# Router logits with the weights stationary in four column groups of TensorE, summed by a second product

## The chip, the cores and the metric

The kernel runs on one core of one Trainium2 chip. The metric is the device time of one execution in microseconds (us), taken as the median of several runs. Before the change it is 1420.48 us (three runs, 1419.78 to 1422.85).

## What is computed

One decoder layer on 256 tokens of width 1024, in float32: three parallel causal mixers (gated DeltaNet, a gated linear recurrence, sliding-window attention), merged and projected; a layer norm; a mixture of 32 experts of which every token uses four; a layer norm; a per-layer embedding; a layer norm. The change lies between the first layer norm and the experts, in the router:

```
x = layer_norm(DEEPNORM_ALPHA * x + y, ln1_g, ln1_b)          # y: the mixers' output, times w_out
logits = (xt @ router_w + router_b).astype(jnp.float32)       # (256, 1024) @ (1024, 32)
top_vals, top_idx = lax.top_k(logits, TOP_K)
gates = jax.nn.softmax(top_vals, axis=-1)
```

Every chosen pair of token and expert gets a seat in that expert's buffer, and the expert's two matrices are applied to the buffer.

## The kernel before

The program has two halves. The **mixer** half runs as a list of "units": each is a batch of matrix products (lines L396 and L406, each float32 operand split into a high and a low part, three products) into a PSUM tile `pjt`, and then a generator that evacuates the result. Beside the units run "strands", generators that are advanced once per unit (`steps` in `run`, L465 to L482). A `yield` in a generator therefore puts what follows it one unit later in the program, and when the units have run out the strands go round in turn until all are finished. The order of the instructions on each engine is fixed when the program is built; an engine executes its own queue strictly in that order.

The last nine units multiply the merged mixer output by `w_out`. The tokens come as two halves of 128 (t = 0, 1), the 1024 output columns as two halves of 512 (c = 0, 1). When one pair (t, c) is complete, `evac` in `out_unit` (L1196 to L1217) adds the residual (L1202, tile `y`), takes its statistics (L1203) and spawns `logits(t, c)` (L1219). That strand turns the 128 x 512 piece by four transposes (L1223), copies it from PSUM to the tile `xT` (L1224, printed under its buffer's name `MG`) on ScalarE, and multiplies it with the router's weights `rw`, whose rows were scaled by the norm's gain earlier (`router_weights`). Four products (L1228) per piece, each with 128 tokens of `xT` stationary and the 32 columns of `rw[:, k]` moving, accumulate the 128 x 32 logits of a half of the tokens in a PSUM bank `M["rps", t]`. The layer norm's mean and scale are put in afterwards, on the logits (L1259, L1260).

`router` (L1241) is one strand for both halves. On VectorE it takes for each t the logits (L1259, L1260), the four largest (L1262 to L1265, the choice goes into `tail`), and after an exponential on ScalarE (L1267) the softmax (L107 to L109). For t = 0 it then multiplies the choice with a triangular matrix (L1272) to count seats, and VectorE makes the seats (L118, L119) and the one-hot matrix `oh` (L113). `first_norm(t)` writes the normed tokens `xs` on ScalarE (L1238).

The **expert** half begins with `group(0)` (L1505): it gathers the seated tokens by products with the one-hot matrices (L1518; t = 0 first, then the seats of t = 1 by L123 to L126, L118, L119, L113, and then the gather with t = 1), scales them into `xe` (L1488), and then every expert does its first product (L1564), activation, second product (L1599) and the spread back (L1622). The weights, 12 MB for each expert, come through ten buffers of 2 MB, issued by SyncE (SP) in order. Two 512 KB transfers for the residual (`ob`, `bd`, L1527) are issued by ScalarE's queue.

Of the kernel before, what the change touches and what calls it, by code (L numbers as in the profile page):

```python
# [8 lines left out]
F32 = mybir.dt.float32  # L9
# [5 lines left out]
ALU = mybir.AluOpType  # L15
# [5 lines left out]
P = 128  # L21
KD = D // P
H = 8
NE = 32
# [39 lines left out]
def body(ctx, tc, nc, a, out, dbg=None):  # L64
    sync, act, dve, pool, pe = nc.sync, nc.scalar, nc.vector, nc.gpsimd, nc.tensor
    dbg = dbg or {}

    con = ctx.enter_context(tc.tile_pool(name="con", bufs=1))
    dram = ctx.enter_context(tc.tile_pool(name="dram", bufs=1, space=DRAM))
    pp = ctx.enter_context(tc.tile_pool(name="pp", bufs=1))  # L70
    cst = con.tile([P, 4 * P], F32, name="cst")
    ones = con.tile([P, P], F32, name="ones")

    con.tile([P, 96], F32, name="padc")
    xs = pp.tile([P, 2, D], F32, name="xs")
    rt = Routing(pp)
    pp.tile([P, 112], F32, name="padp")
    el = ctx.enter_context(tc.tile_pool(name="el", bufs=1))
    with ExitStack() as mx:
        mx.enter_context(tc.manual_schedule(engines=None))  # L80
        early = mixer(mx, tc, nc, a, xs, rt, dram, cst, ones, el)
    if dbg:
        for n, v in (("X1", xs), ("G", rt.G), ("POS", rt.pos)):
            pool.dma_start(dbg[n], v)
    moe(ctx, tc, nc, a, out, dbg, xs, rt, dram, cst, ones, el, early)
# [53 lines left out]
def mixer(mx, tc, nc, a, xs, rt, dram, cst, ones, el):  # L139
# [5 lines left out]
    sync, act, dve, pool, pe = nc.sync, nc.scalar, nc.vector, nc.gpsimd, nc.tensor  # L145
# [6 lines left out]
    m2 = mx.enter_context(tc.tile_pool(name="m2", bufs=2))  # L152
# [40 lines left out]
    rw = mpa.tile([P, KD, NE], F32, name="rw")  # L193
# [3 lines left out]
    mv = mpa.tile([P, 2, 4], F32, name="mv")  # L197
# [7 lines left out]
    def wait(*names):  # L205
        while not all(n in events for n in names):
            yield
# [16 lines left out]
    ident, stri, iota, cmask = (cst[:, i * P:(i + 1) * P] for i in range(4))  # L224
# [269 lines left out]
    M = {}  # L494
# [664 lines left out]
    lc_ = mpa.tile([P, 2, NE], F32, name="lc1")  # L1159

    def router_weights():
        yield from wait("late", "att3")
        col = lambda i: pr[:, 65 + 8 * i:73 + 8 * i].unsqueeze(2).to_broadcast([P, KD, NE])
        rb_ = m2.tile([P, T], F32, name="rwb", tag="sq").rearrange("p (k e) -> p k e", e=NE)
        sums_ = m2.tile([P, T], F32, name="rws", tag="sq").rearrange("p (n e) -> p n e", e=NE)
        dve.tensor_tensor(out=rb_, in0=rw, in1=col(1), op=ALU.mult)
        dve.tensor_reduce(out=sums_[:, 1], in_=rb_.rearrange("p k e -> p e k"), axis=AX.X, op=ALU.add)
        yield
        dve.tensor_tensor(out=rw, in0=rw, in1=col(0), op=ALU.mult)
        dve.tensor_reduce(out=sums_[:, 0], in_=rw.rearrange("p k e -> p e k"), axis=AX.X, op=ALU.add)  # L1170
        yield
        ps = yield from banks.take()
        pe.matmul(ps[:, 0:2 * NE], ones, sums_[:, 0:2].rearrange("p n e -> p (n e)"), start=True, stop=True)
        yield
        dve.tensor_scalar(lc_[:, 0], ps[:, 0:NE], -1.0, None, op0=ALU.mult)
        dve.tensor_add(lc_[:, 1], ps[:, NE:2 * NE], rb)
        banks.done(ps)
# [8 lines left out]
    def out_unit(work, done):  # L1186
# [10 lines left out]
        def evac(_):  # L1197
            for t, c in done:
                if t not in rows:
                    rows[t] = wp.tile([P, KD * P], F32, name="y", tag="w")  # L1200
                y = rows[t][:, halves[c]]
                dve.scalar_tensor_tensor(y, xs[:, t, halves[c]], 2.0 * ALPHA, out_ps[t, c], ALU.mult, ALU.add)  # L1202
                dve.bn_stats(lns[:, t, c], y)  # L1203
                if c == 0 and t == 0:
                    for i in range(2):
                        M["rps", i] = yield from banks.take()
                    M["wk"] = wp.tile([P, KD * P], F32, name="wk", tag="w")
                    pool.memset(M["wk"][:, 0:80], -3.0e38)
                spawn(logits(t, c))
                if c:  # L1210
                    dve.bn_aggr(mv[:, t, 0:2], lns[:, t])
                    dve.tensor_scalar(mv[:, t, 2:3], mv[:, t, 1:2], 4 * LN_EPS, None, op0=ALU.add)
                    pool.tensor_tensor(out=mv[:, t, 2:3], in0=mv[:, t, 2:3], in1=mhalf[:, 0:1], op=ALU.pow)
                    spawn(first_norm(t))
            yield
        return products, evac, ()

    def logits(t, c):

        xT = M["xT"]  # L1220
        b = yield from banks.take()
        for k in range(4):
            pe.transpose(b[:, k * P:(k + 1) * P], rows[t][:, (4 * c + k) * P:(4 * c + k + 1) * P], ident)  # L1223
        act.copy(xT[:, 4 * c:4 * c + 4, t * P:(t + 1) * P], b.rearrange("p (k t) -> p k t", k=4))  # L1224
        banks.done(b)
        yield
        for k in range(4 * c, 4 * c + 4):
            pe.matmul(M["rps", t][:, :NE], xT[:, k, t * P:(t + 1) * P], rw[:, k], start=k == 0, stop=k == KD - 1)  # L1228
        if c:
            events.add(f"r{t}")  # L1230

    def first_norm(t):
# [9 lines left out]
    def router():  # L1242

        yield from wait("r0", "n0")
        wk = M["wk"]
        n = [0]

        def take(c, rows=P):
            n[0] += c
            return wk[:rows, n[0] - c:n[0]]  # L1250
        two = lambda v: v.rearrange("p (t c) -> p t c", t=2)
        lg, mr40 = two(take(80)), two(take(80))
        ex, sel = (take(NE), rt.ex), (rt.sel0, rt.sel)
        m8, m4, sm = two(take(16)), two(take(16)), (take(2), rt.sm)
        pool.memset(m4, -3.0e38)
        for t in range(2):
            if t:
                yield from wait("r1", "n1")
            dve.scalar_tensor_tensor(lg[:, t, :NE], lc_[:, 0], mv[:, t, 0:1], M["rps", t][:, :NE], ALU.mult, ALU.add)  # L1259
            dve.scalar_tensor_tensor(lg[:, t, :NE], lg[:, t, :NE], mv[:, t, 2:3], lc_[:, 1], ALU.mult, ALU.add)  # L1260
            banks.done(M["rps", t])
            dve.max(m8[:, t], lg[:, t, :NE])  # L1262
            dve.tensor_copy(m4[:, t, 0:4], m8[:, t, 0:4])
            dve.match_replace(mr40[:, t], m4[:, t], lg[:, t], imm_value=-1.0e38)
            dve.tensor_tensor(out=sel[t], in0=mr40[:, t, :NE], in1=lg[:, t, :NE], op=ALU.not_equal)  # L1265
            dve.tensor_scalar(sm[t][:, 0:1], m8[:, t, 0:1], -1.0, None, op0=ALU.mult)
            act.activation(ex[t], lg[:, t, :NE], AF.Exp, bias=sm[t][:, 0:1])  # L1267
            if t == 0:
                rt.softmax(dve, 0, ex[0], sel[0], sm[0][:, 1:2])
                yield  # L1270
                ps2 = yield from banks.take()
                pe.matmul(ps2[:, :NE], stri, sel[0], start=True, stop=True)  # L1272
                yield
                rt.seat(dve, 0, ps2[:, :NE], sel[0])
                banks.done(ps2)
                rt.places(dve, iota, 0, 0)
# [87 lines left out]
    spawn(delta(1))  # L1364
    spawn(norm_rows())
    spawn(router_weights())
    spawn(router())
    spawn(prefetch())
    spawn(bias_parts())
# [521 lines left out]
```

## Time and profile before

| | us |
|---|---|
| median of three runs | 1420.48 |
| lowest and highest | 1419.78, 1422.85 |
| the profiled execution's own time | 1418.43 |
| its span, first to last instruction | 1416.70 |

The profile is of one execution. A row of the order of time gives a start, how long the row was busy, the engine, the line, the operation, what is written and read, the shape and how many instructions are merged into it; brackets at the end give the idle time before it and what ended it. PE is TensorE's products, PEld its loads of stationary operands, DVE VectorE, ACT ScalarE. A float32 product appears as two records, so the four products of a piece are a row of eight. The duration of a product's record holds its way through the array, so that rows overlap: the pace is read from one row's start to the next one's. The mixer half ends at about 443 us and the expert half fills the rest to about 1376 us.

### The profile page before, as it was taken

To read this page: it belongs to the slowest core of one execution; us is meant where nothing else is said; L and a number is where in the kernel's file an instruction comes from. 1 tells how busy PE (TensorE), PEld (TensorE's weight loads), DVE (VectorE), ACT (ScalarE), POOL (GpSimd) and SP (SyncE) were. 2 spreads that over 40 slices of the span, in tenths; PEclk is the share of its full clock that TensorE was granted. 3 is DMA by queue.
4 is the path that set the end of the run, shared out by engine and by line. 5 is a ranking of instruction groups with operands and counts; after the bars stand their busy time and mean duration, and the time that the engine had idled before them with its cause. 6 is when DMAs were issued, how large, how long until landed. Compare 5 with 4: busy or idle time off the path is not lost. (4 is left out here: it accounts for less than half of the span.)

```text
span 1416.7 us, 19387 instructions
## 1 busy us (share of the span) xinstructions
PE 1342.9 (95%) x7722; PEld 750.8 (53%) x7723; DVE 591.8 (42%) x1255; ACT 403.1 (28%) x811; POOL 250.0 (18%) x219
## 2 busy tenths in 40 slices
PE   8999989999999999999999999999999999999987
PEld 7989967888886333333333333334333333333326
DVE  6398884876564332223222222223222322222238
ACT  6767464644554111111111111111111111111121
POOL 6654774434561000000000000000000000000000
PEclk9999999999999999999999999999999999999988
DMA  8755455345887999999999999999999999999970
GB/s 263 216 139 137 132 183 170 111 139 181 308 302 281 414 429 431 429 429 428 428 431 429 430 428 427 431 430 429 427 430 430 430 429 427 430 429 430 429 295 30
DMA packets 122198, 481.69 MB, mean 340 GB/s; under 512 B 11403, under 2 KB 69404, under 8 KB 88696
## 3 DMA queue, kind: packets, MB, share of 16 engines
q1 hardware_dynamic: 120440, 477.16, 84.2%
q0 software_dynamic: 912, 1.87, 0.4%
q10 hardware_dynamic: 752, 1.38, 0.3%
q8 instruction: 62, 1.02, 0.3%
q14 instruction: 32, 0.26, 0.0%
HBM read 478.79 MB, written 3.42 MB: 340 GB/s over the span
## 5 line engine op out<-in xcount | busy, mean ns | idle before, releaser
L1564 PE MATMUL gu<-w,xe 128*64 128x512 f32 x1168 | 261.9, 599 | 0.0
L457 POOL TENSOR_TENSOR LO<-w,HI 128x384 fp32r<-128x384 f32 (+1 forms) x113 | 170.6, 1511 | 161.1 <-ACT HI L452 154.8
L1564 PE MATMUL gu<-F,xe 128*64 128x512 f32 x880 | 198.4, 596 | 0.1
L1564 PEld LDWEIGHTS gu<-w,xe 128*64 128x64 f32 x1168 | 82.9, 138 | 156.6 <-issue 153.2
L455 DVE TENSOR_TENSOR LO<-w,HI 128x640 fp32r<-128x640 f32 (+1 forms) x113 | 117.6, 1042 | 81.4 <-ACT HI L452 79.5
L1461 POOL DMA_DIRECT2D pt<-in_p_dram x1 | 0.8, 777 | 779.8 <-DVE lc L1586 779.8
L1627 DVE TENSOR_TENSOR Y<-Y,cb 128x512 f32<-128x512 f32 x128 | 82.1, 682 | 127.5 <-PE cb L1622 127.5
L452 ACT CAST HI<-w 128x1024 fp32r<-128x1024 f32 x113 | 118.0, 1045 | 59.1 <-PE pjt L406 35.1
L1599 PE MATMUL dn<-w,hT 128*64 128x512 f32 x560 | 132.2, 615 | 2.0 <-ACT hT L1592 2.0
L1582 DVE TENSOR_SCALAR gc<-gu 128x256 f32<-128x256 f32 x64 | 26.9, 421 | 249.3 <-PE gu L1564 249.3
L396 PE MATMUL pjt<-xh,HI 128*128 128x256 f32 x424 | 125.9, 297 | 0.0
L396 PE MATMUL pjt<-xh,LO 128*128 128x256 f32 x424 | 121.6, 287 | 1.3 <-DVE LO L455 1.3
L396 PE MATMUL pjt<-xl,HI 128*128 128x256 f32 x424 | 121.2, 286 | 0.0
L1564 PEld LDWEIGHTS gu<-F,xe 128*64 128x64 f32 x880 | 60.8, 137 | 112.8 <-issue 109.8
L1496 PE MATMUL gat<-oh,xs 128*128 128x128 f32 x480 | 72.3, 296 | 37.7 <-DVE oh L113 19.9
L1599 PE MATMUL dn<-F,hT 128*64 128x512 f32 x464 | 106.0, 599 | 0.0
L1583 ACT ACTIVATE sg<-gc 128x256 f32<-128x256 f32 x64 | 27.2, 425 | 274.6 <-DVE gc L1582 274.6
L1496 PEld LDWEIGHTS gat<-oh,xs 128*128 128x128 f32 x480 | 60.9, 199 | 55.4 <-issue 26.4
L396 PEld LDWEIGHTS pjt<-xh,HI 128*128 128x128 f32 x424 | 82.7, 195 | 1.8 <-issue 1.1
L396 PEld LDWEIGHTS pjt<-xh,LO 128*128 128x128 f32 x424 | 82.6, 195 | 2.0 <-DVE LO L455 1.9
L396 PEld LDWEIGHTS pjt<-xl,HI 128*128 128x128 f32 x424 | 82.7, 195 | 0.3
L1599 PEld LDWEIGHTS dn<-w,hT 128*64 128x64 f32 x560 | 38.2, 142 | 74.6 <-issue 63.5
(417 smaller groups left out, 1724.9 us busy)
## 6 DMA issues: line engine op xcount, KB each, us to landing
w<-in_w_gu_dram SPq DMA_DIRECT2D x73, 2048.0 KB, 26.9
F<-in_w_gu_dram SPq DMA_DIRECT2D x51, 2048.0 KB, 28.2
w<-in_w_down_dram SPq DMA_DIRECT2D x70, 1024.0 KB, 21.7
F<-in_w_down_dram SPq DMA_DIRECT2D x58, 1024.0 KB, 22.1
w<-in_w_in_dram SPq DMA_DIRECT2D x85, 512.0 KB, 3.8
F<-in_w_gu_dram SPq DMA_DIRECT2D x8, 1024.0 KB, 6.1
w<-in_w_o_lru_dram SPq DMA_DIRECT2D x8, 512.0 KB, 4.6
w<-in_w_o_swa_dram SPq DMA_DIRECT2D x8, 512.0 KB, 3.7
```

The lines of the kernel that those rows point to most:

```text
L396: pe.matmul(ps, hl[l][:, k * P:(k + 1) * P], b[r][:, k], start=k == 0 and n == 0, stop=k == KD - 1 and n == 2)
L452: act.copy(hi, s)
L455: dve.tensor_sub(lo[:, 0:n], s[:, 0:n], hi[:, 0:n].bitcast(F32))
L457: pool.tensor_tensor(out=lo[:, n:], in0=s[:, n:], in1=hi[:, n:].bitcast(F32), op=ALU.subtract)
L1461: pool.dma_start(pt, a["p"][0, 0].rearrange("(t p) c -> p t c", p=P))
L1496: pe.matmul(ps[:, kk], xs[:, t, k * P:(k + 1) * P], oh[:, t], start=t == 0, stop=t == 1)
L1564: pe.matmul(gu[64 * j:64 * j + 64, b], xe[:, k], w[:, j * D + b * 512:j * D + (b + 1) * 512], start=False, stop=k == KD - 1)
L1582: dve.tensor_scalar(gc[:, c], guv[:, c, 0], 7.0, None, op0=ALU.min)
L1583: act.activation(sg[:, c], gc[:, c], AF.Sigmoid, scale=1.702)
L1599: pe.matmul(dn[64 * jj:64 * jj + 64], hT[:, 2 * hf + kk, j * 64:j * 64 + 64], w[:, kk, jj * 512:(jj + 1) * 512], start=hf == j == kk == 0, ...
L1627: dve.tensor_add(y, y, pss[jj])
```

## The change

The products are turned round: `rw[:, k]` (128 x 32) is stationary and 128 tokens of `xT` move. The four products of a piece go to four groups of 32 columns of the array and so to four groups of 32 partitions of the bank, each holding a partial sum of the logits, transposed (32 experts x 128 tokens). When both pieces of a half are in, ScalarE copies the 128 x 128 partial sums to SBUF (tile `lgp`, L1239 of the changed kernel), and one product with that copy stationary and `sel4` moving (four 32 x 32 identities on top of each other) adds the four groups and turns the logits back to tokens x experts (L1242). `sel4` is built once, in the strand `router_weights`, by three additions on VectorE into a tile that was padding. For t = 0 the copy comes one unit later than the products and the sum one unit after the copy; for t = 1 there is no `yield` between them.

```diff
-    pp.tile([P, 112], F32, name="padp")
+    rt.odd = pp.tile([P, 112], F32, name="odd")
...
     def router_weights():
         yield from wait("late", "att3")
+        M["sel4"] = s4 = rt.odd[:, 16:48]
+        dve.tensor_add(s4, ident[:, 0:32], ident[:, 32:64])
+        dve.tensor_add(s4, s4, ident[:, 64:96])
+        dve.tensor_add(s4, s4, ident[:, 96:128])
...
         banks.done(b)
         yield
-        for k in range(4 * c, 4 * c + 4):
-            pe.matmul(M["rps", t][:, :NE], xT[:, k, t * P:(t + 1) * P], rw[:, k], start=k == 0, stop=k == KD - 1)
+
+        for k in range(4):
+            pe.matmul(M["rps", t][32 * k:32 * k + 32, 0:P], rw[:, 4 * c + k], xT[:, 4 * c + k, t * P:(t + 1) * P], start=c == 0, stop=c == 1)
         if c:
+
+            if t == 0:
+                yield
+            part = m2.tile([P, P], F32, name="lgp", tag="cv")
+            act.copy(part, M["rps", t][:, 0:P])
+            if t == 0:
+                yield
+            pe.matmul(M["rps", t][:, P:P + NE], part, M["sel4"], start=True, stop=True)
             events.add(f"r{t}")
...
-            dve.scalar_tensor_tensor(lg[:, t, :NE], lc_[:, 0], mv[:, t, 0:1], M["rps", t][:, :NE], ALU.mult, ALU.add)
+            dve.scalar_tensor_tensor(lg[:, t, :NE], lc_[:, 0], mv[:, t, 0:1], M["rps", t][:, P:P + NE], ALU.mult, ALU.add)
```

The change also moves work on three engines, because the strand `router` starts on an event that now comes two units later.

**VectorE, around the last piece (t = 1, c = 1).** L1202 and L1203 are that piece's residual and statistics, L1259 (changed kernel: L1272) the first step on the logits of t = 0, L109 the last of its softmax, L118 the first step of its seats. Before:

```order
L1259 SCALAR_TENSOR_TENSOR wk<-lc_150,mv,pg 128x32
L1260 SCALAR_TENSOR_TENSOR wk<-wk,mv,lc_150 128x32
...
L109 TENSOR_SCALAR GP<-wk 128x32
L1202 SCALAR_TENSOR_TENSOR y<-xs,pjt 128x512
L1203 BN_STATS lns<-y 128x6
L1211 BN_AGGR mv<-lns 128x2
L1212 TENSOR_SCALAR mv<-mv 128x1
L118 SCALAR_TENSOR_TENSOR GP<-pg,tail 128x32
```

Here the softmax of t = 0 is over before the last piece's residual begins. With the change:

```order
L1206 SCALAR_TENSOR_TENSOR y<-xs,pjt 128x512
L1207 BN_STATS lns<-y 128x6
L1215 BN_AGGR mv<-lns 128x2
L1216 TENSOR_SCALAR mv<-mv 128x1
L1272 SCALAR_TENSOR_TENSOR wk<-lc_150,mv,pg 128x32
L1273 SCALAR_TENSOR_TENSOR wk<-wk,mv,lc_150 128x32
...
L109 TENSOR_SCALAR GP<-wk 128x32
L1248 SCALAR_TENSOR_TENSOR mv<-mv 128x1
L118 SCALAR_TENSOR_TENSOR GP<-pg,tail 128x32
```

The chain of t = 0 stood ahead of the last piece's residual and now stands behind its statistics.

**ScalarE, at the same place.** L1224 (L1228) are the copies of turned pieces, L1267 (L1280) the exponentials, the first for t = 0 (`wk`), the second for t = 1 (`tail`). Before:

```order
L1224 COPY MG<-pg 128x4x128
L1267 ACTIVATE wk<-wk 128x32
L1224 COPY MG<-pg 128x4x128
L1238 ACTIVATE xs<-y,mv 128x512 x2
L1267 ACTIVATE tail<-wk,tail 128x32
```

The two middle rows are the exponential of t = 0 and, behind it, the last piece's copy. With the change:

```order
L1228 COPY MG<-pg 128x4x128
L1239 COPY lgp<-pg 128x128
L1280 ACTIVATE wk<-wk 128x32
L1228 COPY MG<-pg 128x4x128
L1239 COPY lgp<-pg 128x128
L1251 ACTIVATE xs<-y,mv 128x512 x2
L1280 ACTIVATE tail<-wk,tail 128x32
```

The order of the old instructions is the same, with two copies of partial sums put in; the exponential of t = 0 is still ahead of the last piece's copy.

**TensorE, from the last batch of products on.** L1272 (L1285) counts the seats of t = 0, L1518 (L1531) is the first gather. Before:

```order
L1272 MATMUL pg<-tail,cst 128x32
L1223 MATMUL pg<-cst,y 128x128 x4
L1548 LDWEIGHTS pick
...
L1548 MATMUL gu<-bias,pick 64x512
L1228 MATMUL pg<-rw,MG 128x32 x4
L1518 MATMUL gat<-oh_72,xs 128x128 x8
```

The count of the seats of t = 0 comes first, before the last piece is turned. With the change:

```order
L1242 MATMUL pg<-odd,lgp 128x32
L1227 MATMUL pg<-cst,y 128x128 x4
L1561 LDWEIGHTS pick
...
L1561 MATMUL gu<-bias,pick 64x512
L1285 MATMUL pg<-tail,cst 128x32
L1233 MATMUL pg<-MG,rw 32x128 x4
L1242 MATMUL pg<-odd,lgp 128x32
L1531 MATMUL gat<-oh_72,xs 128x128 x8
```

The sum for t = 0 stands where the count of its seats stood, and that count has moved behind the last piece's transposes and the expert half's first bias products.

## Rows read from the trace of the kernel before

**Rows 1.** Busy time by stretch: us, then PE PEld DVE ACT POOL (instructions), PEclk, DMA share, GB/s

```profile
445.00:450.00 5.00, 3.96 (x37) 3.43 (x33) 3.19 (x20) 3.37 (x5) 0.60 (x2) 1.00 0.98 419
600.00:700.00 100.00, 94.78 (x480) 38.02 (x478) 27.22 (x63) 14.79 (x38) 0.00 (x0) 1.00 1.01 430
```

**Rows 2.** What TensorE waited for from 460 to 1380 us: total, times, longest

```profile
PE gat L1496 <- DVE oh L113: 19.9, 15, 2.1
PE gat L1496 <- ACT xe L1488: 17.9, 30, 0.7
```

**Rows 3.** TensorE in order of time, from the third piece's products on

```profile
440.95 0.97 PE L1228 MATMUL pg<-rw,MG 128*128 128x32 f32 x8
441.76 0.48 PE L406 MATMUL pjt<-RV,AT 128*128 128x512 f32 x1
...
443.24 0.30 PE L1272 MATMUL pg<-tail,cst 128*128 128x32 f32 x2
...
445.51 1.08 PE L1228 MATMUL pg<-rw,MG 128*128 128x32 f32 x8
446.43 2.03 PE L1518 MATMUL gat<-oh,xs 128*128 128x128 f32 x16
448.29 0.31 PE L123 MATMUL seats<-tail,ones 128*128 128x32 f32 x2
...
449.95 1.13 PE L1518 MATMUL gat<-oh,xs 128*128 128x128 f32 x8 [0.92 <-DVE tail L107]
451.18 1.94 PE L1564 MATMUL gu<-F,xe 128*64 128x512 f32 x8
```

**Rows 4.** VectorE in order of time, same place

```profile
439.29 0.25 DVE L1259 SCALAR_TENSOR_TENSOR wk<-lc,mv,pg 128x32 f32<-128x32 f32 x1 [3.33 <-PE pg L1228]
...
441.80 0.24 DVE L109 TENSOR_SCALAR GP<-wk 128x32 f32<-128x32 f32 x1
443.44 0.69 DVE L1202 SCALAR_TENSOR_TENSOR y<-xs,pjt 128x512 f32<-128x512 f32 x1 [1.40 <-PE pjt L406]
...
445.20 0.18 DVE L118 SCALAR_TENSOR_TENSOR GP<-pg,tail 128x32 f32<-128x32 f32 x1
...
445.95 0.16 DVE L1235 SCALAR_TENSOR_TENSOR mv<-mv 128x1 f32<-128x1 f32 x1
446.63 0.25 DVE L1259 SCALAR_TENSOR_TENSOR wk<-lc,mv,pg 128x32 f32<-128x32 f32 x1 [0.52 <-PE pg L1228]
...
449.51 0.29 DVE L113 TENSOR_TENSOR oh<-cst,GP 128x128 f32<-128x128 f32 x1
```

**Rows 5.** ScalarE in order of time, same place and one later cast

```profile
441.01 0.32 ACT L1267 ACTIVATE wk<-wk 128x32 f32<-128x32 f32 x1 [0.66 <-DVE wk L1266]
444.87 0.58 ACT L1224 COPY MG<-pg 128x512 f32<-128x512 f32 x1 [3.54 <-PE pg L1223]
446.15 2.52 ACT L1238 ACTIVATE xs<-y,mv 128x512 f32<-128x512 f32 x2 [0.69 <-DVE mv L1235]
...
458.54 0.37 ACT L1571 CAST gt<-gwt 128x256 fp32r<-128x256 f32 x1 [1.43 <-PE gwt L1570]
```

**Rows 6.** TensorE at 304 us: whole-array products, products in two column groups

```profile
304.20 1.05 PE L916 MATMUL pg<-RV,U 128*128 128x128 f32 x8
305.18 1.52 PE L1082 MATMUL pg<-F 128*64 128x256 f32 x12
```

**Rows 7.** The loads of those products in two column groups

```profile
305.18 1.06 PEld L1082 LDWEIGHTS pg<-F 128*64 128x64 f32 x12
```

**Rows 8.** Clock in one us, columns as in Rows 1

```profile
473.00:474.00 1.00, 1.00 (x4) 0.30 (x4) 0.00 (x0) 0.73 (x2) 0.00 (x0) 0.50 1.09 459
```

**Rows 9.** Gathers of eight records in order of time

```profile
469.38 1.13 PE L1496 MATMUL gat<-oh,xs 128*128 128x128 f32 x8 [2.14 <-DVE oh L113]
...
471.40 1.82 PE L1496 MATMUL gat<-oh,xs 128*128 128x128 f32 x8 [0.66 <-ACT xe L1488]
```

**Rows 10.** SyncE's transfers in order of time

```profile
447.19 0.33 SPq L1421 DMA_DIRECT2D w<-in_w_gu_dram  x1
```

## Prediction

> **What bounds the kernel now.** I read the busy time by stretch first. From 600 to 700 us TensorE is 94.78 us busy of 100 at the full clock, and DMA is full as well, share 1.01 at 430 GB/s [rows 1]. So the second view decides, what TensorE waited for through the whole expert half: VectorE's one-hot matrices, 19.9 us in fifteen waits, and ScalarE's scaled tokens, 17.9 us in thirty; both repeat with the experts, and no wait for a transfer is among the large ones [rows 2]. The weights come just in time, and TensorE's own sequence sets the time. Whatever moves the start of that sequence moves the end by as much.
>
> Then the order of time at the seam. Up to 443 us TensorE's rows follow each other without a gap, so there a shorter product is time saved. From 443.44 us, when VectorE begins the last piece's residual [rows 4], to 449.95 us, when the gather of t = 1 starts [rows 3], a chain through TensorE, ScalarE and VectorE rules: TensorE is 3.96 us busy of 5 [rows 1]. I call the start of that residual y and count from it; the gather of t = 1 stands at y + 6.51 before.
>
> **The products in column groups.** Before, a piece's eight records take 0.81 us, from 440.95 to 441.76 [rows 3]. What eight records with 32 stationary columns in four groups and 128 moving tokens take, no row shows. The nearest rows: eight whole-array records of 128 moving columns take 0.98 us (304.20 to 305.18), 0.12 each, and twelve records in two groups with 256 moving columns are busy 1.52 us, 0.13 each [rows 6]. Twice the columns in the same time: the two groups ran side by side. Four groups at a quarter of 0.98 us give 0.25 us; no side by side gives 0.98. I take 0.40 us, near the lower end, since the row in groups is the nearest, with 0.15 us for turning the array from whole to groups and back. Three of the four pieces stand in the gapless stretch: 3 x (0.81 - 0.40) = **1.2 us saved** (between 1.7 saved and 0.5 lost). The sum for t = 0 takes the place of the count of its seats, 0.30 us then [rows 3], and an equal product now: nothing. The three additions for `sel4` run on VectorE far earlier, a few tenths of a microsecond in a stretch in which TensorE is the full engine: nothing.
>
> The page "TensorE: Matmul & The Clock Gate" of the Trainium skill (Part 3, The mechanism) speaks against this: a weight load overlaps a running product only if the row group differs, and here all four groups use all rows. The trace shows the loads of the two-group products busy for 1.06 us [rows 7] of the same 1.5 us in which the products ran; so here they did overlap. What the rule would give is a rival below.
>
> **What waits now at the seam.** The logits of t = 0 used to be worked on from 439.29 to 442.04 us (L1259 to the end of L109, 2.75 us), inside the gapless stretch and ahead of y [rows 4]. In the changed order their sum comes after the last batch of products, and VectorE reaches them only behind the last piece's residual and statistics. The instruction behind those started at 445.20, y + 1.76 [rows 4]; now the chain of t = 0 starts there. Its exponential on ScalarE started 1.72 us into the chain and took 0.32 us (441.01 [rows 5]), so it ends at y + 1.76 + 2.04 = y + 3.80.
>
> ScalarE's queue is strict, and that exponential stands ahead of the last piece's copy. The copy started at 444.87, y + 1.43, before [rows 5]; now it waits until y + 3.82 and ends, after 0.58 us, at y + 4.40. That is the step on which the forecast rests: **a wait of 2.4 us on ScalarE** for a copy that everything behind it needs. From there:
> - The products follow 0.06 us behind the copy (445.45 to 445.51 before) and took 1.12 us until VectorE had the logits at 446.63 [rows 3, 4]; with 0.41 us less, 0.71: y + 5.17.
> - The copy of the partial sums, 128 columns. A cast of 256 columns took 0.37 us and a copy of 512 took 0.58 [rows 5], so about 0.27, with 0.04 for the hand-over: y + 5.48.
> - The sum: 0.15 us until a product starts on fresh data (449.51 + 0.29 to 449.95 [rows 3, 4]), 0.30 as L1272 [rows 3], 0.04 to VectorE: the logits of t = 1 at y + 5.97. Before, y + 3.19.
>
> VectorE is free by then: the chain of t = 0 ends at y + 4.51, and its seats and one-hot matrix (445.20 to 446.11 before, 0.91 us [rows 4]) at y + 5.42. The first gather follows the sum on TensorE and starts 2.8 us later than before, at y + 5.8; it takes 1.86 us (446.43 to 448.29 [rows 3]), and the seats and the second gather come behind it as before. ScalarE writes `xs` for t = 1 in 2.52 us [rows 5] from y + 5.45 and is done at y + 8.0, before the second gather needs it at y + 9.3. **The seam grows by 2.8 us** (2.4 if the products and the copy cost no more than the old products, 3.4 if the groups save nothing).
>
> SyncE's transfer at 447.19 [rows 10] waits for VectorE's last read of the norm's constants for t = 1 and comes about 1.6 us later (2.8 less 1.2). DMA has earlier 2 MB still in hand, at 419 GB/s [rows 1], and the weights it brings are used an expert later: nothing.
>
> **The clock.** In one place TensorE stood idle 2.14 us, ran a gather, stood idle 0.66 us [rows 9], and then the granted clock was 0.50, the level of 1.2 GHz, in the stretch shown [rows 8]; the gather under it took 1.82 us for eight records where 1.13 stood [rows 9]. In the longer seam TensorE has next to nothing from y + 2.1 (445.51, where the last piece's products used to follow the bias products [rows 3]) to y + 4.46, then two short bursts. So I expect the fall here too, in the first gather: sixteen records, twice 0.69 = 1.4 us if all of it is under the fall, 0 if none. I take **1.1 us**, near the upper end.
>
> **The sum.** -1.2 + 2.8 + 1.1 = +2.7 us, against the profiled execution's 1418.43: 1421.1. That execution stood 2.05 us under the median, and the difference carries over: 1420.48 + 2.7, rounded down for what the falls elsewhere may give back, **1423.1 us**. The bound of 0.2%, about what a measurement of this kernel can tell from no change, is 2.84 us, 1423.32: the forecast lies just inside it. The main case has 0.46, from 1422.2 to 1424.2, of which 0.30 lies inside the bound and 0.16 above.
>
> **Rivals.**
> - The clock holds. For it: 600 to 700 us has gathers with waits and a clock of 1.00 [rows 1]. Then +1.6: 1422.1. Chance 0.21, within 0.2%.
> - Slower: the fall lasts through the second gather and the first products of expert 0 as well. These are eight gather records (1.13 us) and eight products (1.94 us) [rows 3], some 1.5 us more at half the clock. For it: the seam has two idle places, at y + 2.1 and before the second gather. It decides if the clock is still at 0.50 at y + 10. +4.2: 1424.7. Chance 0.13.
> - The change doesn't do what it says: the groups take turns. Then a piece takes 0.98 us, 0.5 us is lost in three pieces and 0.6 us in the seam's own products: 0.5 + 2.8 + 0.6 + 1.1 = +5.0, 1425.5. Against it: [rows 6]. With loads that do not overlap either, 0.09 us for a load (1.06 by 12 [rows 7]) and 0.12 for a record, eight of each take 1.7 us: 2.6 lost in three pieces, 1.3 in the seam, +7.8, 1428.3. Together 0.09, slower. The second is what the skill's rule above would make of it.
> - DMA sets the end, and the seam's wait is covered by it, while the first big transfer, which waits for the last batch of products, comes 1.2 us earlier: 1419.3 to 1420.5. For it: DMA share 1.01 [rows 1]; against it: [rows 2]. Chance 0.08, within 0.2%.
> - Falls of the clock that stand elsewhere in the trace of before do not come again with the new timing. Each costs about what the gather shows, 0.7 us and the products behind it as much: three fewer than before (4.5 us), with the clock holding at the seam, make 1.6 - 4.5 = -2.9: 1417.6. Chance 0.03, faster.
>
> **How the numbers follow.** Faster 0.03, rounded up to 0.04; within 0.2%: 0.30 + 0.21 + 0.08 = 0.59, rounded to 0.57; slower: 0.16 + 0.13 + 0.09 = 0.38, rounded to 0.39. The range leaves out the groups taking turns, the faster case and most of the DMA case: 1421.0 to 1425.2.
>
> **What would show it.** Right: in the changed profile the batch behind a piece's products starts about 0.4 us after them instead of 0.81; the exponential of t = 0 ends some 3.8 us after y and the last piece's copy starts right behind it; the second gather starts near y + 9.3, or y + 10.4 with the clock at 0.50; from there on the trace of before repeats, shifted. Wrong: if the last piece's copy starts near y + 1.4, the main term is gone and the change is faster by a microsecond; if a piece's products take 0.8 us or more, the saving is; if TensorE waits for transfers in the expert half, the seam does not count in full.

## The result, and the profile after

The changed kernel takes **1437.05 us** (median of 4, 1435.37 to 1437.69); beside it on the same chip the kernel before took 1420.35 (median of 4). The ratio is 1.0109, 95% interval 1.0095 to 1.0124: slower by 15.5 us by that ratio (the two medians lie 16.7 apart), against +2.7 forecast, and outside the range. The profiled execution took 1436.83 us with a span of 1435.1, 18.4 us more than the span of before.

The order of time comes first, beside [rows 3, 4, 5]. TensorE in the trace of after, from the third piece's products on, with the product ahead of them and an earlier one, ahead of the first piece's products (columns as there):

```profile
432.08 0.48 PE L406 MATMUL pjt<-HI,AT 128*128 128x512 f32 x1
...
440.72 0.40 PE L406 MATMUL pjt<-KT,AT 128*128 128x512 f32 x1
441.04 0.43 PE L1233 MATMUL pg<-MG,rw 128*32 128x128 f32 x8
441.40 0.50 PE L406 MATMUL pjt<-RV,AT 128*128 128x512 f32 x1
...
447.42 0.66 PE L1233 MATMUL pg<-MG,rw 128*32 128x128 f32 x8 [0.30 <-ACT MG L1228]
448.46 0.64 PE L1242 MATMUL pg<-odd,lgp 128*128 128x32 f32 x2 [0.39 <-ACT lgp L1239]
448.90 3.76 PE L1531 MATMUL gat<-oh,xs 128*128 128x128 f32 x16
...
454.30 1.13 PE L1531 MATMUL gat<-oh,xs 128*128 128x128 f32 x8 [0.92 <-DVE tail L107]
```

The same two products in the trace of before:

```profile
431.36 0.48 PE L406 MATMUL pjt<-HI,AT 128*128 128x512 f32 x1
...
440.72 0.39 PE L406 MATMUL pjt<-KT,AT 128*128 128x512 f32 x1
```

The loads for the third piece's products, of after and of before:

```profile
441.04 0.16 PEld L1233 LDWEIGHTS pg<-MG,rw 128*32 128x32 f32 x8 [0.36 <-issue]
```

```profile
440.73 1.09 PEld L1228 LDWEIGHTS pg<-rw,MG 128*128 128x128 f32 x8
```

ScalarE at the same place of after, the exponential of t = 0, the last piece's copy and the copy of its partial sums:

```profile
446.57 0.32 ACT L1280 ACTIVATE wk<-wk 128x32 f32<-128x32 f32 x1 [6.07 <-DVE wk L1279]
446.80 0.56 ACT L1228 COPY MG<-pg 128x512 f32<-128x512 f32 x1
448.14 0.27 ACT L1239 COPY lgp<-pg 128x128 f32<-128x128 f32 x1 [0.78 <-PE pg L1233]
```

VectorE at the same place of after, the last piece's residual y and the first step on the logits of t = 0 and of t = 1:

```profile
443.10 0.69 DVE L1206 SCALAR_TENSOR_TENSOR y<-xs,pjt 128x512 f32<-128x512 f32 x1 [6.42 <-PE pjt L406]
...
444.86 0.24 DVE L1272 SCALAR_TENSOR_TENSOR wk<-lc,mv,pg 128x32 f32<-128x32 f32 x1
...
449.13 0.25 DVE L1272 SCALAR_TENSOR_TENSOR wk<-lc,mv,pg 128x32 f32<-128x32 f32 x1 [0.82 <-PE pg L1242]
```

A piece's products take 0.36 us (441.04 to 441.40) instead of 0.81. They start 0.32 us behind the product ahead of them (440.72), 0.09 later than before, so that a piece saves 0.36 us: from that product to the batch behind the piece it is 0.68 us, before 1.04. With three such pieces, y comes 11.02 us behind the product at 432.08, and before 12.08 us behind the same one at 431.36: 1.06 us earlier. At the seam, y is now 443.10. The chain of t = 0 starts at y + 1.76, its exponential ends at y + 3.79, the last piece's copy follows at y + 3.70 (before: y + 1.43), the logits of t = 1 come at y + 6.03. The first gather takes 3.76 us where 2.03 stood. The second starts at 454.30, y + 11.2, which is 4.35 us after that of before. The clock did fall at this place; busy time by stretch of after, columns as in [rows 1]:

```profile
447.00:449.00 2.00, 1.32 (x12) 0.75 (x11) 1.17 (x8) 1.23 (x3) 0.00 (x0) 0.50 0.00 0
418.00:460.00 42.00, 38.19 (x212) 28.24 (x211) 18.82 (x59) 15.08 (x25) 7.27 (x9) 0.92 0.27 101
```

So far this is the seam as forecast, a little longer. It accounts for some 4 of 18.4 us. The second of these rows shows where the rest begins: from 418 to 460 us the transfers moved 101 GB/s. The same stretch of the kernel before:

```profile
418.00:460.00 42.00, 40.22 (x226) 29.74 (x226) 19.34 (x60) 16.85 (x26) 6.87 (x9) 1.00 0.74 291
```

(291 - 101) GB/s x 42 us = **8.0 MB** that have not arrived at 460 us, when the expert half has just begun. SyncE's transfers in order of time, of before:

```profile
405.27 12.27 SPq L445 DMA_DIRECT2D w<-in_w_out_dram  x6
417.76 17.50 SPq L1433 DMA_DIRECT2D w<-in_w_down_dram  x4
```

and of after:

```profile
449.12 1.99 SPq L1446 DMA_DIRECT2D w<-in_w_down_dram  x4
451.16 10.26 SPq L1434 DMA_DIRECT2D w<-in_w_gu_dram  x4
```

These are the expert half's first transfers into its buffers `w`, and they leave 31.4 us later. (8 MB of the first expert's weights, issued by L1141 up to 392 us into the other buffers `F`, come early in both.) Below, "first transfer" means the one at 417.76 or 449.12. What SyncE waited for (total, times, longest), of after:

```profile
SPq L1434 <- DMA w<-in_w_gu_dram: 312.8, 70, 5.3
...
SPq L1434 <- DMA F<-in_w_gu_dram: 204.0, 45, 5.8
...
SPq L1446 <- PE pg L1242: 30.7, 1, 30.7
...
SPq L1434 <- PE dn L1612: 1.0, 4, 0.3
```

and of before:

```profile
SPq L1421 <- PE dn L1599: 182.0, 46, 10.1
SPq L1421 <- DMA w<-in_w_gu_dram: 154.7, 46, 4.6
SPq L1433 <- PE gu L1564: 135.4, 48, 5.6
```

One wait of 30.7 us for L1242, the sum of the partial logits. The tile `lgp`, which that sum reads, was put into the slot "cv" of the pool `m2`, memory of the mixer half that was free by then, and that memory becomes the weight buffer of this first transfer. A transfer may overwrite `lgp` only when its last reader is done, and every other transfer stands behind it in SyncE's queue. The large waits are of another kind too: before, SyncE often waited for TensorE to give a buffer back (182.0 us for the second products alone); after, that is 1.0 us, and what is left is waits for earlier transfers. In the kernel before the kind of wait turns with time: from 460 to 600 us all but 0.9 us of them are for TensorE (122.0 us, the buffers are full), from 1200 to 1340 us only 3.2 us are. Accordingly TensorE now waits for weights (its waits from 460 to 1380 us; before there is no such line, and [rows 2] stand unchanged beside these):

```profile
PE gu L1577 <- DMA F<-in_w_gu_dram: 6.1, 8, 1.2
PE gu L1577 <- DMA w<-in_w_gu_dram: 4.6, 7, 1.2
```

How 8 MB can matter so late is seen in the pace of the experts and of the transfers. The second activation of the first expert on ScalarE and the same one thirty experts later, in order of time, of before:

```profile
471.50 0.43 ACT L1583 ACTIVATE sg<-gc 128x256 f32<-128x256 f32 x1
...
1334.98 0.42 ACT L1583 ACTIVATE sg<-gc 128x256 f32<-128x256 f32 x1
```

and of after:

```profile
475.84 0.43 ACT L1596 ACTIVATE sg<-gc 128x256 f32<-128x256 f32 x1
...
700.17 0.43 ACT L1596 ACTIVATE sg<-gc 128x256 f32<-128x256 f32 x1
...
1353.20 0.42 ACT L1596 ACTIVATE sg<-gc 128x256 f32<-128x256 f32 x1
```

Busy time by stretch within the expert half, columns as in [rows 1], of before and of after:

```profile
600.00:1300.00 700.00, 670.46 (x3300) 263.64 (x3296) 182.08 (x415) 100.53 (x252) 0.78 (x1) 0.99 1.01 429
600.00:1300.00 700.00, 661.43 (x3232) 257.91 (x3228) 179.87 (x410) 98.92 (x248) 0.78 (x1) 0.99 1.01 429
```

Before, an expert takes 863.48 / 30 = 28.78 us. Its 12 MB (12 x 1.0486 = 12.58 million bytes) take 29.3 us at 429 GB/s. **The transfers are the slower of the two**, and the expert half lives on a stock that was brought in while the mixers were still running; before, it lasts to the end, since no wait for weights is seen. After, an expert takes 877.36 / 30 = 29.25 us. That is a mean over two stages: the first eight experts take 28.0 us each (475.84 to 700.17), on the smaller stock, and the other 22 take 29.7. TensorE's first wait for weights stands at the border:

```profile
721.72 3.65 PE L1577 MATMUL gu<-w,xe 128*64 128x512 f32 x16 [0.74 <-DMA w<-in_w_gu_dram]
```

The experts begin 4.3 us later (475.84 - 471.50) and thirty of them take 13.9 us more, together 18.2 of the 18.4 us. This says where the time lies, not that a shorter seam would give 4.3 us back: the run with the slot and no delay, below, has a shorter seam and takes as long. Falls of the clock are not the cause either: read in stretches of 2 us from 460 to 1380 us, the trace of after has five of them, and that of before seven. Counted as time x (1 - granted clock), they cost 10.2 and 13.8 us.

### The profile page after: what moved, and what is told of

Same layout as the page of the kernel before. It is cut to its first block, busy times and chain, and to the rows that moved or that the text cites. A ratio compares the mean times of both kernels' runs of the same rounds, so it can differ in the third digit from the quotient of the medians.

```text
span 1435.1 us, 19399 instructions
## 1 busy us (share of the span) xinstructions
PE 1346.0 (94%) x7726; PEld 746.1 (52%) x7727; DVE 596.3 (42%) x1258; ACT 402.9 (28%) x813; POOL 248.7 (17%) x219
## 3 DMA queue, kind: packets, MB, share of 16 engines
HBM read 478.79 MB, written 3.42 MB: 336 GB/s over the span
## 6 DMA issues: line engine op xcount, KB each, us to landing
F<-in_w_gu_dram SPq DMA_DIRECT2D x51, 2048.0 KB, 29.3
```

## The experiments

Theory M: the time goes with the memory in which `lgp` stands, through the first transfer. Theory S: it goes with the order of the work at the seam, and the late transfer is covered.

**The copies in other memory.** The 128 x 128 copy is put into columns of `xT`, already read by the products, with all delays kept:

```diff
-            part = m2.tile([P, P], F32, name="lgp", tag="cv")
+            part = xT[:, t, 0:P]
```

> The changed kernel with one edit: the copies of the partial sums stand in a part of xT that has been read for the last time, no longer in a slot of the pool m2. Theory M (the slot's memory becomes the first weight buffer of the expert half, so the first transfer waits for the sum of t = 1): the first w_down transfer is issued near 418 us again, TensorE no longer waits for transfers, and only the longer seam is left, 4.35 us in the trace of the change (second gather at 454.30 instead of 449.95), so 1420.4 + 4.4 = about 1424.8; 1422.0 to 1425.5. Theory S (the longer seam with its fall of the clock delays everything behind it, and the late transfer is only carried along): the seam is the same, so 1435 to 1437.

Measured: 1425.67 us (10 runs), ratio 1.0022 (1.0002 to 1.0041). The first weight transfer is at 419.44 us and TensorE waits for no weights. The seam's rows are those of the change, the clock's fall included. The time is 0.2 us above what theory M allowed. So 12 of the 15.5 us lost were the memory's (14.6 by the second timing of this kernel, below).

**The memory without the change.** The kernel before, with nothing but its 16-column scratch `m4` in that slot; the router is untouched, and the scratch's last reader works on the logits of t = 1:

```diff
-        m8, m4, sm = two(take(16)), two(take(16)), (take(2), rt.sm)
+        m8, m4, sm = two(take(16)), two(m2.tile([P, P], F32, name="m4c", tag="cv")[:, 0:16]), (take(2), rt.sm)
```

> The kernel before with one edit and no added instruction: the router's scratch m4 (16 columns, last read by VectorE for t = 1 near 448 us) stands in a slot of m2 instead of in wk. Theory M: the first w_down transfer waits until about 448 us instead of 418 and the time rises by nearly as much as with the change, to 1433 to 1437. Theory S: the seam is that of before, so 1420.4, within 1 us.

Measured: 1436.04 us, ratio 1.0114 (1.0097 to 1.0131), as slow as the change. What its SyncE waited for:

```profile
SPq L1433 <- DVE wk L1264: 30.2, 1, 30.2
```

and SyncE in order of time in the same run:

```profile
446.82 2.28 SPq L1433 DMA_DIRECT2D w<-in_w_down_dram  x4
```

The seam of this run is that of before. The slot alone makes the whole loss; theory S falls.

**One delay taken out, with the memory freed and with the slot kept.** Both take out the `yield` between the products of t = 0 and their copy; the first also has the copies in `xT`:

```diff
-            if t == 0:
-                yield
             part = xT[:, t, 0:P]
```

> As e1, and one of the two pauses for t = 0 taken out (the copy follows the products at once, the sum one unit later), so that VectorE does the logits of t = 0 ahead of the last piece's residual again. Both theories of the seam: the copy of the last piece starts about 1.4 us after the residual's start as before, the seam grows only by the copy and the sum less the shorter products (0.27 + 0.04 + 0.49 - 0.45 = +0.35), and three pieces save 0.45 us each less 0.2 for the sum of t = 0: -1.15. Theory M: -0.8, 1419.6, 1419 to 1421. Theory S: the same 1419 to 1421. It tells the part of the seam in e1 from the rest: e1 minus e3 should be about 4 to 5 us.

> The changed kernel with only the order mended (one pause for t = 0, as in e3), the copies still in the slot of m2. Theory M: the first transfer waits for the sum of t = 1, which now comes at about 446 us instead of 448.5, so the time falls by about 2 to 3 us to 1434 to 1435 and no more, although the seam is some 4 us shorter. Theory S: the seam is mended, so 1419 to 1421.

Measured: 1421.16 us, ratio 1.0002 (0.9993 to 1.0012), with the memory free; 1435.97, ratio 1.0109 (1.0093 to 1.0126), with the slot. The slot costs 15 us with or without the delay. With the slot the delay is worth nothing, although the second gather comes at y + 8.28 instead of y + 11.20, and the time is a microsecond above what theory M expected; with the memory free it is worth 0.6 to 2.8 us by the two timings of the kernel with both delays. In the first of the two the clock holds in the first gather (2.03 us; in the second, with the same work there, 3.42), but TensorE now stands idle ahead of the third piece's products, whose copy queues behind the writing of `xs` on ScalarE (TensorE in order of time):

```profile
444.17 0.42 PE L1233 MATMUL pg<-MG,rw 128*32 128x128 f32 x8 [1.27 <-ACT MG L1228]
```

That is the microsecond that the groups had saved.

**Half the lateness.** The kernel with free memory and no delay, but the copy for t = 0 in the slot again:

```diff
-            part = xT[:, t, 0:P]
+            part = xT[:, t, 0:P] if t else m2.tile([P, P], F32, name="lgp", tag="cv")
```

> The run with free memory and no delay (1421.2), but the copy for the first half of the tokens (t=0) stands in the slot that becomes the first weight buffer, the one for t=1 in the unused columns. Theory M (the first weight transfer waits for the last reader of that memory): its last reader is now the sum of t=0, about 441 us, so the transfer leaves some 7 us earlier than in the changed kernel (447 to 449) and 21 to 23 us later than in the kernel before (417.8). If the loss follows the delay in proportion, (441 - 418) / (449 - 418) of 16 us, the time is 1430 to 1434; if the expert half bears the first part of the delay without loss, it is less, 1425 to 1430. Theory S (what costs is the order of the last piece at the end of the router): nothing there changes, so 1420 to 1423.

Measured: 1427.34 us, ratio 1.0047 (1.0032 to 1.0063). SyncE in order of time in this run:

```profile
441.51 1.98 SPq L1444 DMA_DIRECT2D w<-in_w_down_dram  x4
```

and what it waited for:

```profile
SPq L1432 <- PE dn L1610: 67.1, 18, 11.6
...
SPq L1444 <- PE pg L1240: 22.8, 1, 22.8
```

The first transfer leaves where theory M put it, 23.8 us late, and SyncE's waits for the second products are down from 182.0 to 67.1 us. The loss is less than in proportion: the 7.6 us more lateness of the change cost 8.8 us, the first 23.8 cost 6.7. The bytes missing from 418 to 460 us must be brought at 429 GB/s, and they tell the runs that lose time from those that do not. (Left out are the three timings of kernels whose times fall in two groups, below; they moved 288 to 292 GB/s.)

| run | first transfer, us | GB/s 418 to 460 | MB short of before | us at 429 GB/s | loss by the ratio, us |
|---|---|---|---|---|---|
| last piece direct (below) | 419.90 | 288 | 0.1 | 0.3 | 0.1 |
| memory free, no delay | 420.12 | 278 | 0.5 | 1.3 | 0.3 |
| copy of t = 0 in the slot | 441.51 | 184 | 4.5 | 10.5 | 6.7 |
| before, scratch in the slot | 446.82 | 117 | 7.3 | 17.0 | 16.2 |
| slot, no delay | 447.82 | 118 | 7.3 | 16.9 | 15.5 |
| the change | 449.12 | 101 | 8.0 | 18.6 | 15.5 |

The loss is 0.8 to 3.8 us less than the missing bytes' time. That the stock had this much to spare fits, but is not shown: the last three rows do not differ beyond the noise (about 2 us either way), and their order is not that of the bytes.

**The last piece as before.** The kernel with free memory and no delay, in which the last piece is made by four direct products onto the sum of the piece ahead of it, so that no copy stands behind it. It was meant to be faster than both kernels:

```diff
+        if t and c:
+            for k in range(4, KD):
+                pe.matmul(M["rps", t][:, P:P + NE], xT[:, k, t * P:(t + 1) * P], rw[:, k], start=False, stop=k == KD - 1)
...
-            pe.matmul(M["rps", t][:, P:P + NE], part, M["sel4"], start=True, stop=True)
+                pe.matmul(M["rps", t][:, P:P + NE], part, M["sel4"], start=True, stop=t == 0)
```

> This is the changed kernel with its copy of the four partial results in the unused columns of the tile of transposed rows, with the one unit of delay removed, and with the last of the four pieces made as before, by eight products onto the sum of the piece ahead of it. Theory M (the 16 us come from the memory of the copy alone): the first weight transfer leaves at 417 to 421 us, and the time is that of the run with free memory and no delay (1421.2) less the last piece's sum and its copy behind the end of the products, plus its 0.45 us of slower products: 1418 to 1421. Theory S (a product in groups pays its saving back in waits on ScalarE, here for the copy of the third piece): the same or up to 2 us above the kernel before, 1420 to 1423. Both exclude a first transfer later than 425 us.

Measured: 1420.06 us beside 1420.5, ratio 1.0001 (0.9992 to 1.0010): the same. From y (445.87) to the second gather it takes 6.51 us, as before, and the idle 1.27 us ahead of the third piece's products is here too. It lies in the range of both theories; a gain of a microsecond can't be told from none.

**The seam's main term.** The change with its copies in `xT` and its delays, and the exponential of t = 0 moved behind the last piece's copy on ScalarE; and the first experiment once more beside it, unchanged, since its times had fallen in two groups:

```diff
+            if t == 0:
+                yield
             act.activation(ex[t], lg[:, t, :NE], AF.Exp, bias=sm[t][:, 0:1])
```

> The changed kernel with its copies of partial results in free memory and its delays kept, but the exponential of t=0 put behind the last piece's copy on ScalarE. Theory Q (the prediction's main term: the copy's wait of 2.4 us behind that exponential is what lengthens the seam): the copy starts at y+1.4 instead of y+3.7, the second gather comes some 2.4 us earlier, at y+8.8 instead of y+11.2, and the time is 2 to 3 us below that of the same kernel without this edit. Theory D (the chain of t=0 on VectorE, which now begins behind y, sets the first gather by itself, and the wait of the copy lies beside it): the copy starts at y+1.4 as well, but the first gather stays at y+5.4 to y+5.8 and the second within 0.6 us of y+11.2 if the clock falls, and the time is within 1 us of the same kernel without the edit.

> The changed kernel with its copies in the unused columns of the transposed rows and both delays kept, once more, since its ten times lay in two groups (1418 to 1421 and 1425 to 1428). Theory Q and theory D both put it where the prediction's seam does, 1421 to 1426, with the first weight transfer at 417 to 421 us; that the seam costs nothing once the memory is free would be a median within 0.7 us of the kernel before.

Measured: 1419.37 us, ratio 1.0001 (0.9984 to 1.0019), and 1422.09, ratio 1.0006 (0.9988 to 1.0024), 12 runs each. The times do not decide, since both kernels have two groups (1415.6 to 1421 and 1423 to 1427). The trace of the moved exponential does, in part. ScalarE in order of time in that run (y is 440.83):

```profile
442.26 0.58 ACT L1228 COPY MG<-pg 128x512 f32<-128x512 f32 x1 [4.03 <-PE pg L1227]
444.24 0.32 ACT L1282 ACTIVATE wk<-wk 128x32 f32<-128x32 f32 x1 [1.39 <-DVE wk L1279]
444.47 0.24 ACT L1239 COPY MG<-pg 128x128 f32<-128x128 f32 x1
```

and TensorE there:

```profile
446.22 3.50 PE L1533 MATMUL gat<-oh,xs 128*128 128x128 f32 x16 [0.83 <-DVE oh L113]
...
451.21 1.13 PE L1533 MATMUL gat<-oh,xs 128*128 128x128 f32 x8 [0.92 <-DVE tail L107]
```

The copy starts at y + 1.43, its wait is gone, and the first gather still starts at y + 5.39, 0.4 us earlier than in the change, after a wait for VectorE's one-hot matrix. The second is at y + 10.38 against y + 11.20. In the two traces of the same kernel without this edit it is at y + 11.20 and y + 11.23. This is theory D, with 0.8 us where it allowed 0.6: of the seam's growth by 4.7 us (y + 6.51 to y + 11.20) the copy's wait is 0.8 us; the rest is set by the chain of t = 0 on VectorE, which now runs between y and the first gather, and by the clock, whose fall still makes the first gather slow (3.50 us).

The two groups lie in the clock. In all 24 executions timed here the mean granted clock is 0.985 or more in the lower group and 0.981 or less in the upper one. In the expert half, read as above, the profiled execution of 1427.54 us has seven falls, which cost 15.3 us, and that of 1415.57 us three, which cost 5.1. The difference is 10.2 of the 12.0 us between their spans. One place has a fall in both, at products that use a single row of the array (`1*128`). TensorE in order of time in the kernel with the copies in `xT`, an execution of 1427.54 us:

```profile
833.10 4.18 PE L1717 MATMUL cb<-w,ones 1*128 1x512 f32 x8
837.21 8.23 PE L1577 MATMUL gu<-F,xe 128*64 128x512 f32 x24
```

and with the exponential moved, one of 1415.57 us:

```profile
827.34 3.69 PE L1719 MATMUL cb<-w,ones 1*128 1x512 f32 x8
830.97 7.07 PE L1579 MATMUL gu<-F,xe 128*64 128x512 f32 x24
```

That is 1.65 us at one place (4.18 + 8.23 against 3.69 + 7.07). These products alone do not bring it: in the traces of before and of the change the clock holds behind them, and the 24 products take 5.37 us. What decides on a fall and its length no run here shows, nor whether the seam has a part in it.

## Why the prediction was wrong

- **The products in groups: right.** 0.40 us forecast, 0.36 measured, or 0.45 with the 0.09 us by which they start later. Three pieces were to save 1.2 us, and y came 1.06 us earlier. The 0.15 us for turning the array was an allowance that no row gave: the traces show the 0.09 us on the way in and none on the way back. The page "TensorE: Matmul & The Clock Gate" of the Trainium skill (Part 3, The mechanism) lets loads overlap products only where the row group differs; the trace disagrees within the piece, since four groups that share all rows ran eight records in 0.36 us, where the prediction's estimate without overlap is 1.7. On the way in it agrees: the first load begins only with the groups' own first product, at 441.04, where before it began at 440.73, beside the product of 440.72.
- **The seam: right in its times, too short by 0.8 us, and in part for the wrong reason.** Every start up to the logits of t = 1 came within 0.15 us (y + 1.76, 3.79, 3.70, 6.03). The second gather was forecast for y + 10.4 with the clock at 0.50 and came at y + 11.2; the fall took 1.7 us in the first gather, 3.76 instead of 2.03, and stretched the sum as well (0.64 instead of 0.30). That the logits of t = 1 came so near is in part luck: the clock was at 0.50 by then, and the last piece's products took 0.72 us up to the copy (447.42 to 448.14), where 0.71 was forecast at the full clock; with the clock held, in the run with free memory and no delay, it is 0.49. That ScalarE's wait of 2.4 us is what lengthens the seam is not borne out: taking it away moved the second gather by 0.8 us, since VectorE's chain of t = 0 lies beside it. With the memory free the whole is worth +0.1% by the two timings (1.0022 and 1.0006); the forecast's +2.7 us is a ratio of 1.0019 and lies in both intervals. The second interval holds no change at all as well, so the times neither confirm nor refute the seam's part of the sum.
- **The transfers: the step that failed.** The prediction put it so: "SyncE's transfer at 447.19 [rows 10] waits for VectorE's last read of the norm's constants for t = 1 and comes about 1.6 us later … and the weights it brings are used an expert later: nothing." It looked at a transfer that waits for the router anyway and costed the queue at nothing from that one row. It did not ask which memory the new tile takes and who gets it next. The first transfer, at 417.76 us, was some 30 us ahead of the router's end and now waits for it; in its place stands a term of 8.0 MB, 18.6 us at 429 GB/s, of which 15.5 us are measured as loss.
- **What bounds the kernel: misread, and this is why the sum had no term for the transfers.** "The weights come just in time, and TensorE's own sequence sets the time" was read from [rows 2], where no wait for a transfer is large. DMA's share of 1.01 at 430 GB/s in [rows 1] said the other half: the transfers were saturated and slower than TensorE by half a microsecond for each expert. No wait was seen only because a stock was being used up. What SyncE waited for shows it: in the kernel before it turns from TensorE to transfers in the course of the expert half. The page "DMA: Bandwidth & Descriptors" of the Trainium skill (Where 436 GB/s comes from) gives a ceiling of 435 GB/s; the trace agrees with 429 from 600 to 1300 us, before and after. The same section lets the HBM side bind at about 358 GB/s for transfers such as these; the trace disagrees, with the same 429. With the transfers at 429 without a pause, a late byte is not made up, apart from what the stock spares.
- **The rivals.** That DMA sets the end was among them with 0.08, but with the first big transfer coming *earlier*, and so on the other side. The fall of the clock came, with 1.7 us in the first gather where 1.1 was taken; it did not last through the second gather (1.13 us), and the groups did not take turns. "If TensorE waits for transfers in the expert half" was named as a sign that the seam does not count in full: it was seen, and it held, since with the slot a shorter seam changed nothing. What it left out is that the transfers themselves had become later, which costs more than the seam.

## What to carry to other kernels

A new tile costs more than the instructions that touch it: ask which memory it takes, who is next in that memory, and what is queued behind that one; for an in-order queue the first wait is the price of all behind it. And "no waits for transfers" beside a DMA share of 1 does not mean that the transfers keep up. Divide the bytes of a step by the rate and compare with the step's own time: if the transfers are slower, a stock is being spent, and a byte that comes late at the start is paid at the end, once the stock has nothing to spare.

## What the hardware showed that was not expected

- Eight records of four column groups over all 128 rows took 0.36 us, 0.045 each, where eight whole-array records of as many moving columns took 0.98 [rows 6]: more than twice as fast. Going from the whole array to groups cost 0.09 us (440.72 to 441.04, where 0.23 is the pace of those products); going back cost nothing that can be read (the next product follows at 441.40).
- The granted clock falls to 0.50, the level of 1.2 GHz, also while TensorE is busy without a gap. In the kernel with the copies in `xT`, busy time by stretch, 1 us behind the start of the 24 products above:

```profile
838.00:842.00 4.00, 4.00 (x12) 1.18 (x10) 0.00 (x0) 0.00 (x0) 0.00 (x0) 0.50 1.01 434
```

Ahead of it stood 4 us of products that use a single row of the array (the record at 833.10), not idle time; the places known before the prediction were idle ones [rows 8, 9].
